# Weight loads in program order, side work fenced behind low halves, and three sets of transposes moved from TensorE to VectorE with a bounce through DRAM

## The chip, the cores and the metric

One core of one Trainium2 chip runs the kernel. The metric is the device time in microseconds (us) of one execution. PE is TensorE (matmuls and transposes by matmul), DVE is VectorE, ACT is ScalarE, POOL is GpSimd and SP is SyncE; SP and POOL only issue DMAs in most of this kernel.

## What is computed

One layer of a streaming encoder on 256 frames of width 2048, all in float32, cut here to what matters:

```
h  = rms_norm(x);  p = h @ w_in            # columns: x_m 1024 | out gate 1024 | u 512 | branch gates 4096
xc = silu(conv4(x_m)); q, k = xc per head; v = x_m per head     # 4 heads of 256
hcell = chunkwise mLSTM(q, k, v, gates)    # matrix memory with max stabiliser
y_m = (sigmoid(o_pre) * (norm(hcell) * g + skip * xc)) @ w_up_m
s   = associative scan of 32 groups x 64 complex states of u    # S5
y   = gelu(Re(C s) + D u);  y_s = (y * sigmoid(y @ w_glu + b)) @ w_up_s
x   = x + (sigmoid(g_m) * y_m + sigmoid(g_s) * y_s) @ w_out
h2  = rms_norm(x);  x = x + (silu(h2 @ w_gate) * (h2 @ w_up)) @ w_down
out = rms_norm(x)
```

## The kernel before

The weights come in 432 blocks of 128x1024 float32 (512 KB). Each block B0 to B431 takes the same way: SP loads it into a tile `raw` (`emit_dma`), ACT casts it to float32r as `hi`, DVE subtracts `lo = raw - hi` (`emit_split`), and PE multiplies it in three passes, xh·hi, xh·lo and xl·hi, where xh and xl are the same split of the activations: 12 matmuls of 128x512 for a block (24 of 128x256 for the first chunk and for the q, k, v and glu blocks). There are three raw, three hi and three lo buffers; the split of a block is emitted two blocks ahead of its matmuls, its load five ahead. In the FFN every fourth raw lies in the pool u8 instead, which has ten buffers of its own.

The order of blocks: the input projection's chunk 4 (the S5 input u, B0 to B7), chunks 0 and 1 (x_m), branch gates with v, q and k between (v is B40 and B41, q B50 and B51, k B60 and B61), chunks 2 and 3 (the output gate), the other gates. The glu blocks B107 and B108 stand three blocks before the end of the last gate chunk, whose last three blocks are B109 to B111. B112 to B119 project S5's output up (`ups_mm`), B120 to B135 the mLSTM's (`upm_mm`), B136 to B167 are w_out, and the FFN begins at FFN0 = B168.

Beside this main row two generators carry the branches: `s5_gen` (scan, output matmuls `y_mm`, GELU, glu) and the mLSTM's `ml_gen`. After each block `pump` lets them emit steps worth a budget of DVE time; the numbers that a step yields are its cost on DVE, its cost on PE and how many blocks must pass before the next. At some places a block needs the result and calls `until`, which emits all that is missing at once. The compiler then schedules each engine's instructions by their dependences: the row on an engine need not be the row of emission, and work without an order between may overtake. Once emitted, each engine runs its row strictly in order. `tc.issue_after(x)` lets what is emitted under it stand only behind instruction x on its engine. Before the change, pump used it in one place only, for S5 steps behind the last of the gates' instructions (`state["fence"]`).

S5's last stretch are the "fix products": 32 elementwise DVE instructions of 128x960 on `stm` and `bu`, in four quarters; behind each quarter eight matmuls of `y_mm` (`aux<-bu,s5sp`, two groups), an addition into `s5ud`, and after the second and the fourth quarter GELU. The split of that, `ghl`, is what the glu blocks multiply.

PE also transposes by matmul with the identity: v (16 of 128x128, into `vtok`), and in `ml_gen`'s last part the heads' output `hc` and the output gate `so` (32). For the merged branches and for x1 the kernel transposes otherwise: DVE transposes 32x32 blocks (`blocks_T`), and POOL's queue writes the tile to DRAM and reads it back in four pieces that put the blocks in place (`groups_dma`, the bounce).

Of the kernel before, what the change touches and what calls it, by code (L numbers as in the profile page):

```python
# [13 lines left out]
AF = mybir.ActivationFunctionType  # L14
# [3 lines left out]
P = 128  # L18
# [22 lines left out]
NTAIL = 5  # L41
# [6 lines left out]
def block_kernel(ctx: ExitStack, tc: tile.TileContext, d, out):  # L48
    nc = tc.nc
# [35 lines left out]
    def aux():  # L85
        return pp.tile([P, 512], F32, tag="aux", name=nm("aux"), bufs=4)
# [6 lines left out]
    def TT(o, a, b, op):  # L93
        return V.tensor_tensor(o, a, b, op=op)  # L94
# [7 lines left out]
    def f(ap):  # L102
        return ap.bitcast(F32)
# [27 lines left out]
                blocks.append((d[name][n, kp], fn_maker, (n, kp)))  # L131

    raws, splits = {}, {}
    wdma = [None]

    def emit_dma(i):
        if i < len(blocks):
            if i == 3:
                raw = u32([P, 1024], name="raw")
            elif FFN0 + 4 <= i < len(blocks) - NTAIL - 4 and i % 4 == 3:  # L140
                raw = u8([P, 1024], name="raw")
            else:
                raw = wp.tile([P, 1024], F32, tag="raw", name=nm("raw"), bufs=NRAW)
            wdma[0] = nc.sync.dma_start(raw, blocks[i][0]).ins
            raws[i] = raw

    def emit_split(i):
        if i < len(blocks):
            raw = raws.pop(i)
            if i >= len(blocks) - NTAIL:  # L150
                hl = u8([P, 2, 1024], F32R, name="hl")
                hi, lo = hl[:, 0], hl[:, 1]
            else:
                hi = wp.tile([P, 1024], F32R, tag="hi", name=nm("hi"), bufs=NHI)
                lo = wp.tile([P, 1024], F32R, tag="lo", name=nm("lo"), bufs=NHI)
            A.copy(hi, raw)  # L156
            TT(lo, raw, f(hi), SUB)
            splits[i] = (hi, lo)

    def o2_block(acc, lhs, kts, hi, lo, first, last):  # L160
# [47 lines left out]
    def pump(i, budget, share, pe=PEB):  # L208
        debt[0] += budget + side_pe[0]
        side_pe[0] = 0.0  # L210
        debt[2] += pe
        while debt[0] > 0 and debt[2] > 0:
            live = [g for g in gens if not g.done and g.ok <= i]
            if not live:
                break
            if len(live) == 2 and debt[1] > 0:
                live.reverse()
            c = None
            for g in live:
                if g is gens[0] and "fence" in state:  # L220
                    with tc.issue_after(state["fence"]):
                        c = g.step()
                else:
                    c = g.step()
                if c:
                    break
                g.ok = i + 1
            if not c:
                break
            dv, p, lat = (tuple(c) + (0, 0))[:3] if isinstance(c, tuple) else (c, 0.0, 0)  # L230
            g.ok = i + lat
            debt[0] -= dv
            debt[2] -= p
            side_pe[0] += p
            debt[1] += dv * (1 - share) if g is gens[0] else -dv * share
        debt[0] = min(debt[0], 0.0)
        debt[2] = min(debt[2], 0.0)
        debt[1] = max(-3.0, min(3.0, debt[1]))
# [39 lines left out]
    def groups_dma(dt_, st_):  # L278
        w = st_.shape[2]
        bounce = dp_.tile([P, 4, w], F32, tag=f"d{w}", name=nm("bounce"))  # L280
        nc.gpsimd.dma_start(bounce, st_)  # L281
        for j in range(4):
            nc.gpsimd.dma_start(  # L283
                dt_[32 * j : 32 * j + 32], bounce.rearrange("(i r) j x -> r i j x", i=4)[:, :, j]
            )


    s5 = {}
# [240 lines left out]
    def ml_gen():  # L529
# [38 lines left out]
        vk = u16([P, 2, 2048], name="vk")  # L568
        ml["vk"] = vk
        vtok = vk[:, 0].rearrange("p (a b) -> p a b", a=2)  # L570
        for st in range(2):
            for e4 in range(2):
                ps_ = aux()
                for e in range(4):
                    PE.transpose(ps_[:, e * 128 : e * 128 + 128], vT[:, e4 * 4 + e, st * 128 : st * 128 + 128], ident)
                A.copy(vtok[:, st, e4 * 512 : e4 * 512 + 512], ps_)
                yield 0.05, 0.45, e4
        gt = cp.tile([P, 2, 8], F32, name="gt")


# [5 lines left out]

        def gate_part(i, src, base):
            gs = m2([P, 256])
            nc.gpsimd.memset(gs, 0.0)
            ps_ = aux()  # L590
            for c in range(8):
                r = 32 * (c % 4)
                mm(ps_[r : r + 8, 0:256], wif[:, i * 8 + c, :], src[:, c, :], c < 4, c >= 4)
            for r in range(0, 128, 32):
                A.copy(gs[r : r + 8, :], ps_[r : r + 8, 0:256])
            yield 0.05, 1.2, 1
            pg = aux()
            for tt in range(2):
                mm(pg[:, tt * 8 : tt * 8 + 8], gs[:, tt * 128 : tt * 128 + 128], sel, True, True)
            TT(gt, pg[:, 0:16].rearrange("p (a b) -> p a b", a=2), base, ADD)  # L600
            yield 0.2, 0.4

        yield from gate_part(2, vT, pvs("bif").unsqueeze(1).broadcast_to([P, 2, 8]))
        del vT
        yield 0.2
        xch = u8([P, 8, 256], F32R, name="xch")
        xcl = u8([P, 8, 256], F32R, name="xcl")
# [14 lines left out]
        qT = ml["q"]  # L622
        yield from gate_part(0, qT, gt)
        yield 0.2
        while "k" not in state:
            yield 0
        yield 0.01, 0, 1
# [18 lines left out]
            STT(rc, rc, c, w2, ADD, MUL)  # L646
        STT(rc, rc, 1.0, w, ADD, MUL)
        TS(v3(lf), fg, 0.0, None, MIN)
        state["fence"] = STT(lf, rc, -2.0, lf, MUL, ADD).ins
        yield 2.6  # L650
        state["gates"] = 1
        mneg = cp.tile([P, 4, 2], F32, name="mneg")
# [5 lines left out]
        for hp in range(2):  # L658
# [79 lines left out]
            yield 0.01, 0.65, 1  # L738
            for pT, h in zip(pTs, hh2):
                nps = aux()  # L740
                vs = lambda st: vtok[:, st, h * 256 : h * 256 + 256]
                mm(nps[:, 0:256], pT[:, 0], vs(0), True, True)
                mm(nps[:, 256:512], pT[:, 1], vs(0), True, False)
                mm(nps[:, 256:512], pT[:, 2], vs(1), False, True)
                for tt in range(2):
                    o = hc[:, 2 * h : 2 * h + 2, tt, :]
                    nv = nps[:, tt * 256 : tt * 256 + 256].rearrange("p (a b) -> p a b", a=2)
                    A.activation(o, nv, AF.Copy, scale=dinv[:, h, tt : tt + 1])
                    jk = m2([P, 2, 128])
                    A.activation(jk, o, AF.Square, accum_out=ssh[:, h, tt : tt + 1])  # L750
                yield 0.01, 1.3, 0
# [5 lines left out]
        for h in range(4):  # L757
            for tt in range(2):
                o = hc[:, 2 * h : 2 * h + 2, tt, :]
                A.activation(o, o, AF.Copy, scale=rsh[:, h, tt : tt + 1])  # L760
        yield 0.6, 0, 3
        while "win" not in state:
            yield 0
        so = ml["so"]
        oh = u8([P, 8, 256], F32R, name="oh")
        ol = u8([P, 8, 256], F32R, name="ol")
        for c2 in range(4):
            hps, sps = aux(), aux()
            for src, ps_ in ((hc, hps), (so, sps)):
                for cc in range(2):  # L770
                    for tt in range(2):
                        ct = 2 * c2 + cc
                        c = (cc * 2 + tt) * 128
                        PE.transpose(ps_[:, c : c + 128], src[:, ct, tt, :], ident)  # L774
            t = m2()
            for cc in range(2):
                ct = 2 * c2 + cc
                ts_ = t[:, cc * 256 : cc * 256 + 256]
                A.activation(ts_, xcT[:, ct, :], AF.Copy, scale=pvs("skip", ct))
                STT(ts_, hps[:, cc * 256 : cc * 256 + 256], pvs("mh", ct), ts_, MUL, ADD)  # L780
            TT(t, t, sps, MUL)
            v2 = lambda a: a[:, 2 * c2 : 2 * c2 + 2, :].rearrange("p a b -> p (a b)")
            A.copy(v2(oh), t)
            TT(v2(ol), t, f(v2(oh)), SUB)
            yield 2.1, 0.9, 1
        ml["out"] = (oh, ol)
        state["out"] = 1
        yield 0.1
# [11 lines left out]
    def win_evac(n, acc):  # L800
# [17 lines left out]
                state["xm"] = 1  # L818
        elif n < 4:
            if n == 2:  # L820
                ml["so"] = u8([P, 8, 2, 128], name="so")
            for tt in range(2):
                A.activation(
                    ml["so"][:, 4 * (n - 2) : 4 * (n - 2) + 4, tt, :],
                    acc[tt].rearrange("p (a b) -> p a b", a=4),
                    AF.Sigmoid,
                    scale=r1[:, tt : tt + 1],
                )
            if n == 3:
                state["so"] = 1  # L830
        else:
            c = n - 5
            key, cc = ("gm", c) if c < 4 else ("gs", c - 4)
            if c == 0:
                mlg.until("heads")
            if cc == 0:
                cur[key] = u16([P, 2, 2048], name=key)
            bg = cur["bg"]
            for tt in range(2):
                o = gate_ap(key, tt, cc)  # L840
                STT(o, acc[tt], r1[:, tt : tt + 1], bg, MUL, ADD)
                A.activation(o, o, AF.Sigmoid)
# [518 lines left out]
```

## Time and profile before

| | |
|---|---|
| median of 3 runs | 1253.72 us (1252.34 to 1253.78) |
| the profiled execution's own time | 1254.09 us |
| its span | 1252.2 us |
| granted TensorE clock, mean | 0.997 of full |
| PE busy | 1231.2 us (98%), 5738 matmuls |
| DVE busy | 804.8 us (64%) |
| ACT busy | 604.5 us (48%) |
| POOL busy | 106.7 us (9%) |
| DMA moved | 258.19 MB, 206 GB/s mean |

The span runs from the first to the last instruction in the trace; the execution's own time lies some 2 us above it. Matmuls are pipelined: one of 128x512 lasts 390 ns in the trace, while the next starts long before its end, so a pace is read from the chain of work, which merges a run of matmuls into a start, a length and a count, and not from single durations. DVE's instructions overlap by about a tenth of a microsecond too. Idle time on an engine counts only where PE waits for it.

### The profile page before, as it was taken

The page shows a single profiled execution, that of the slowest core. Times are in us where ns is not written, and L with a number is a line of the kernel's source. Part 1 is how long each engine was busy: PE and PEld are TensorE (multiplying, and loading weights), DVE is VectorE, ACT ScalarE, POOL GpSimd, SP SyncE. Part 2 cuts the span into 40 slices and gives each one's busy share as a digit, 9 for nine tenths or more (in the row PEclk, how much of TensorE's full clock was granted, in tenths as well). Part 3 has the DMA queues.
Part 4 walks back from the last instruction along what each step waited for, and adds up shares of the span by engine and source line. Part 5 has one row for each costly group of instructions (what it writes and reads, how often), then busy time and mean ns, then how long its engine had stood idle before and what let it go on. Part 6 is the DMA issues. An engine that isn't in the chain of part 4 may idle for free.

```text
span 1252.2 us, 15688 instructions
## 1 busy us (share of the span) xinstructions
PE 1231.2 (98%) x5738; PEld 1015.3 (81%) x5738; DVE 804.8 (64%) x1162; ACT 604.5 (48%) x752; POOL 106.7 (9%) x199
## 2 busy tenths in 40 slices
PE   7999999999999999989999999999999999999997
PEld 7877888887788888878888888888888888888885
DVE  8779945899877857646555555655555554554544
ACT  7574554546754445545344444444444443443433
POOL 0000000000000513201101101110111010000000
PEclk9999999999999999999999999999999999999999
DMA  7645655544565888877767766655765686666453
GB/s 264 208 134 185 193 179 190 169 152 150 180 192 179 274 272 280 281 258 224 218 205 227 221 216 210 195 192 197 242 227 183 220 286 193 204 194 201 149 162 141
DMA packets 75597, 258.19 MB, mean 206 GB/s; under 512 B 10496, under 2 KB 11264, under 8 KB 75520
## 3 DMA queue, kind: packets, MB, share of 16 engines
q1 hardware_dynamic: 67616, 237.25, 59.0%
q0 software_dynamic: 7904, 19.94, 4.9%
q8 instruction: 45, 0.74, 0.2%
q14 instruction: 32, 0.26, 0.1%
HBM read 245.09 MB, written 12.06 MB: 205 GB/s over the span
## 4 chain that ended last, share of the span: by engine, by line
PE 90%; DVE 4%; DMA 3%; issue 1%; ACT 1%; POOL 0%; ACTq 0%; SPq 0%; DVEq 0%
PE acc L100 85%; PE aux L100 4%; DVE lo L94 2%; DMA raw<-in_w_out_dram 1%; DMA raw<-in_w_ffn_gate_dram 1%; DVE xcT L97 1%; ACT hi L156 1%; DVE stm L94 1%; DVE bu L94 0%; DMA m<-bounce 0%; DMA raw<-in_w_in_dram 0%; POOL m L283 0%; PE aux L774 0%; DVE xcT L94 0%; DVE x L94 0%
## 5 line engine op out<-in xcount | busy, mean ns | idle before, releaser
L94 DVE TENSOR_TENSOR lo<-raw,hi 128x1024 fp32r<-128x1024 f32 x427 | 521.8, 1223 | 395.8 <-ACT hi L156 395.1
L156 ACT CAST hi<-raw 128x1024 fp32r<-128x1024 f32 x427 | 449.7, 1054 | 571.9 <-PE acc L100 494.1
L100 PE MATMUL acc<-lo,h2h 128*128 128x512 f32 x704 | 274.5, 390 | 0.5 <-DVE lo L94 0.5
L100 PE MATMUL acc<-hi,h2l 128*128 128x512 f32 x704 | 274.5, 390 | 0.0
L100 PE MATMUL acc<-hi,h2h 128*128 128x512 f32 x704 | 246.3, 390 | 2.6 <-ACT hi L156 2.6
L100 PE MATMUL acc<-hi,aT 128*128 128x512 f32 x664 | 204.6, 389 | 0.0
L100 PEld LDWEIGHTS acc<-hi,h2h 128*128 128x128 f32 x704 | 132.6, 188 | 30.5 <-ACT hi L156 3.1
L100 PEld LDWEIGHTS acc<-lo,h2h 128*128 128x128 f32 x704 | 132.4, 188 | 28.6 <-DVE lo L94 1.0
L100 PE MATMUL acc<-lo,hTh 128*128 128x512 f32 x384 | 153.6, 400 | 1.3 <-DVE lo L94 1.2
L100 PEld LDWEIGHTS acc<-hi,h2l 128*128 128x128 f32 x704 | 132.5, 188 | 27.5
L100 PE MATMUL acc<-hi,hTl 128*128 128x512 f32 x384 | 150.5, 392 | 0.0
L100 PEld LDWEIGHTS acc<-hi,aT 128*128 128x128 f32 x664 | 124.6, 188 | 26.0
L100 PE MATMUL acc<-hi,hTh 128*128 128x512 f32 x384 | 139.4, 393 | 0.0
L100 PE MATMUL acc<-lo,aT 128*128 128x512 f32 x332 | 129.1, 389 | 0.0
L100 PEld LDWEIGHTS acc<-lo,hTh 128*128 128x128 f32 x384 | 72.1, 188 | 22.2 <-DVE lo L94 4.0
L100 PEld LDWEIGHTS acc<-hi,hTh 128*128 128x128 f32 x384 | 71.7, 188 | 16.7 <-issue 2.0
L100 PEld LDWEIGHTS acc<-hi,hTl 128*128 128x128 f32 x384 | 72.2, 188 | 14.6 <-issue 0.7
L281 POOL DMA_DIRECT2D bounce<-m x30 | 17.0, 566 | 690.5 <-DVE m L274 688.5
L100 PEld LDWEIGHTS acc<-lo,aT 128*128 128x128 f32 x332 | 62.3, 188 | 12.8
L283 POOL DMA_DIRECT2D m<-bounce x120 | 65.7, 554 | 44.3 <-DMA bounce<-m 27.3
L100 PE MATMUL acc<-lo,mTh 128*128 128x512 f32 x128 | 49.9, 390 | 0.5 <-DVE lo L94 0.5
L100 PE MATMUL acc<-hi,mTl 128*128 128x512 f32 x128 | 49.8, 389 | 0.0
(246 smaller groups left out, 1078.4 us busy)
## 6 DMA issues: line engine op xcount, KB each, us to landing
raw<-in_w_in_dram SPq DMA_DIRECT2D x104, 512.0 KB, 3.5
raw<-in_w_ffn_gate_dram SPq DMA_DIRECT2D x88, 512.0 KB, 4.1
raw<-in_w_ffn_up_dram SPq DMA_DIRECT2D x88, 512.0 KB, 4.4
raw<-in_w_ffn_down_dram SPq DMA_DIRECT2D x88, 512.0 KB, 4.1
raw<-in_w_out_dram SPq DMA_DIRECT2D x32, 512.0 KB, 4.9
raw<-in_w_up_m_dram SPq DMA_DIRECT2D x16, 512.0 KB, 3.6
bounce<-m POOLq DMA_DIRECT2D x30, 256.0 KB, 4.3
m<-bounce POOLq DMA_DIRECT2D x120, 64.0 KB, 4.2
```

What stands on the lines that cost most here:

```text
L94: return V.tensor_tensor(o, a, b, op=op)
L97: return V.scalar_tensor_tensor(out=o, in0=a, scalar=s, in1=b, op0=op0, op1=op1, **kw)
L100: return PE.matmul(o, l, r, start=start, stop=stop, skip_group_check=True)
L156: A.copy(hi, raw)
L281: nc.gpsimd.dma_start(bounce, st_)
L283: nc.gpsimd.dma_start(dt_[32 * j : 32 * j + 32], bounce.rearrange("(i r) j x -> r i j x", i=4)[:, :, j])
```

## The change

1. **Loads.** Every load of a weight block is ordered behind the load of the block before it. Raws in the pool u8 begin at FFN0 + 20 instead of FFN0 + 4.
2. **Side work.** Each step that pump emits stands behind `vlast`, the low half emitted last (that is, of the block two ahead). The single fence at the gates goes. Steps emitted in `until` are not bound.
3. **Transposes.** v, the heads' output and the output gate are transposed as the other tensors are: 4 bounces each (`bounce_T`: one DVE transpose, one write, four reads), 12 in all, instead of 48 matmuls and four ACT copies. The bounce leaves frames in another order, and the matmuls and products that read the tiles take permuted views. v's bounces stand behind q's gate sums, so v's own tile lives until then. The memset of the gate sums moves from POOL to DVE.

```
-    wdma = [None]
+    wdma, vlast = [None], [None]
-            elif FFN0 + 4 <= i < len(blocks) - NTAIL - 4 and i % 4 == 3:
+            elif FFN0 + 20 <= i < len(blocks) - NTAIL - 4 and i % 4 == 3:
-            wdma[0] = nc.sync.dma_start(raw, blocks[i][0]).ins
+            with tc.issue_after(wdma[0]) if wdma[0] else ExitStack():
+                wdma[0] = nc.sync.dma_start(raw, blocks[i][0]).ins
-            TT(lo, raw, f(hi), SUB)
+            vlast[0] = TT(lo, raw, f(hi), SUB).ins
-                if g is gens[0] and "fence" in state:
-                    with tc.issue_after(state["fence"]):
-                        c = g.step()
-                else:
+                with tc.issue_after(vlast[0]):
                     c = g.step()
+    def bounce_T(o, i):
+        st_ = m2([P, 4, 4, 32])
+        V.transpose(st_.rearrange("p j a c -> p a j c"), i.rearrange("p a (j c) -> p a j c", j=4))
+        groups_dma(o.rearrange("p (i x) -> p i x", i=4), st_.rearrange("p j a c -> p j (a c)"))
...
-                for e in range(4):
-                    PE.transpose(ps_[:, e * 128 : e * 128 + 128], vT[:, e4 * 4 + e, st * 128 : st * 128 + 128], ident)
-                A.copy(vtok[:, st, e4 * 512 : e4 * 512 + 512], ps_)
...
-            nc.gpsimd.memset(gs, 0.0)
+            V.memset(gs, 0.0)
...
         yield from gate_part(0, qT, gt)
         yield 0.2
+        for st in range(2):
+            for e4 in range(2):
+                bounce_T(vtok[:, st, e4 * 512 : e4 * 512 + 512], vT[:, 4 * e4 : 4 * e4 + 4, st * 128 : st * 128 + 128])
+                yield 0.75
...
-        state["fence"] = STT(lf, rc, -2.0, lf, MUL, ADD).ins
+        STT(lf, rc, -2.0, lf, MUL, ADD)
...
-        yield 0.6, 0, 3
+        yield 0.6, 0, 1
+        hcd = u8([P, 2, 2, 512], name="hcd")
+        for hh in range(2):
+            for tt in range(2):
+                bounce_T(hcd[:, hh, tt], hc[:, 4 * hh : 4 * hh + 4, tt, :])
+                yield 0.75
+        yield 0.01, 0, 3
...
-            hps, sps = aux(), aux()
-            for src, ps_ in ((hc, hps), (so, sps)):
-                for cc in range(2):
-                    for tt in range(2):
-                        PE.transpose(ps_[:, c : c + 128], src[:, ct, tt, :], ident)
...
-                STT(ts_, hps[:, cc * 256 : cc * 256 + 256], pvs("mh", ct), ts_, MUL, ADD)
-            TT(t, t, sps, MUL)
+                tv = ts_.rearrange("p (i c) -> p i c", c=32)
+                STT(tv, dv_(hcd, ct), pvs("mh", ct), tv, MUL, ADD)
+                TT(tv, tv, dv_(so, ct), MUL)
...
-                A.activation(
-                    ml["so"][:, 4 * (n - 2) : 4 * (n - 2) + 4, tt, :],
...
+                sg = t2()
+                A.activation(sg, acc[tt], AF.Sigmoid, scale=r1[:, tt : tt + 1])
+                bounce_T(ml["so"][:, n - 2, tt], sg.rearrange("p (a c) -> p a c", a=4))
```

The change moves instructions as well. In these rows a name's number only tells tiles apart, and one number does not mean the same tile before and after.

DVE, at the low half of B109, before the change. `lo_3189`, `lo_3207` and `lo_3232` belong to B107, B108 and B109, `ghl` is the split that glu multiplies:

```order
L94 TENSOR_TENSOR lo_3189<-raw_3116,hi_3188 128x1024
L97 SCALAR_TENSOR_TENSOR t_3263<-t_3263,s5ud 128x512
L94 TENSOR_TENSOR lo_3207<-raw_3136,hi_3206 128x1024
L94 TENSOR_TENSOR ghl_3271<-s5ud,ghl_3271 128x512
L94 TENSOR_TENSOR lo_3232<-raw_3164,hi_3231 128x1024
L94 TENSOR_TENSOR lo_3305<-raw_3186,hi_3304 128x1024
L94 TENSOR_TENSOR s5ud<-s5ud,sgt_3270 128x512
```

DVE at the same low half after the change; it is `lo_3284` now, and the low half of B110 is `lo_3382`:

```order
L94 TENSOR_TENSOR lo_3284<-raw_3213,hi_3283 128x1024
L94 TENSOR_TENSOR bu_668<-bu_668,stm_930 128x64x15 x2
L94 TENSOR_TENSOR stm_930<-s5sp_166 128x960 x2
L94 TENSOR_TENSOR bu_668<-bu_668,stm_930 128x64x15
L97 SCALAR_TENSOR_TENSOR s5ud<-s5ud,pv,aux_3291 128x256
L94 TENSOR_TENSOR lo_3382<-raw_3231,hi_3381 128x1024
L94 TENSOR_TENSOR bu_668<-bu_668,stm_930 128x64x15
L94 TENSOR_TENSOR stm_930<-s5sp_166 128x960
L91 TENSOR_SCALAR t_3305<-t_3305 128x512
L94 TENSOR_TENSOR stm_930<-s5sp_166 128x960
L94 TENSOR_TENSOR bu_668<-bu_668,stm_930 128x64x15
L94 TENSOR_TENSOR t_3305<-t_3305,s5ud 128x512
```

Both halves of `ghl` stood ahead of B109's low half before; now fix products stand behind it (five ahead of B110's low half, six ahead of B111's, five ahead of B112's and two behind that), and `ghl` comes later still.

PE, at the end of B106 before the change. `hi_3166` is B106, `hi_3188` is B107, the first glu block:

```order
L100 MATMUL acc_3123<-hi_3166,hTh_79 128x512
L100 MATMUL acc_3123<-lo_3167,hTh_79 128x512
L100 MATMUL acc_3123<-hi_3166,hTl_81 128x512
L100 MATMUL aux_3276<-ghl_3271,hi_3188 128x256
L100 MATMUL aux_3277<-ghl_3271,hi_3188 128x256
L100 MATMUL aux_3276<-ghl_3271,hi_3188 128x256
```

PE after the change, further on, at the end of B111 (`hi_3415`); B107 is `hi_3233` now:

```order
L100 MATMUL acc_3178<-hi_3415,hTh_79 128x512
L100 MATMUL acc_3178<-lo_3416,hTh_79 128x512
L100 MATMUL acc_3178<-hi_3415,hTl_81 128x512
L100 MATMUL aux_3330<-bu_668,s5sp_166 32x256 x4
L100 MATMUL aux_3353<-ghl_3348,hi_3233 128x256 x2
L100 MATMUL aux_3353<-ghl_3348,lo_3234 128x256
```

B107 has moved from behind B106 to behind B111 and the fifth of six groups of `y_mm` that now stand between B106 and B108; B108 follows the sixth.

SP, at the entry to the FFN before the change. `raw_4726` is the block whose matmuls come next behind those of `raw_4702`; the five between lie in the pool u8:

```order
L144 DMA raw_4684<-in_w_ffn_gate_dram 128x1024
L144 DMA raw_4702<-in_w_ffn_gate_dram 128x1024
L144 DMA raw_4788<-in_w_ffn_up_dram 128x1024
L144 DMA raw_4868<-in_w_ffn_up_dram 128x1024
L144 DMA raw_4942<-in_w_ffn_up_dram 128x1024
L144 DMA raw_5022<-in_w_ffn_gate_dram 128x1024
L144 DMA raw_5117<-in_w_ffn_gate_dram 128x1024
L144 DMA raw_4726<-in_w_ffn_gate_dram 128x1024
```

SP at the same place after the change:

```order
L145 DMA raw_4725<-in_w_ffn_gate_dram 128x1024
L145 DMA raw_4743<-in_w_ffn_gate_dram 128x1024
L145 DMA raw_4767<-in_w_ffn_gate_dram 128x1024
L145 DMA raw_4799<-in_w_ffn_up_dram 128x1024
L145 DMA raw_4829<-in_w_ffn_up_dram 128x1024
```

The loads now stand in the order in which their blocks are used.

## Rows read from the trace of the kernel before

**Rows 1.** The page, busy time by engine: us, share of the span, instructions.

```profile
PE 1231.2 (98%) x5738; PEld 1015.3 (81%) x5738; DVE 804.8 (64%) x1162; ACT 604.5 (48%) x752; POOL 106.7 (9%) x199
```

**Rows 2.** PE's waits: who waited for whom, us in total, times, longest.

```profile
PE acc L100 <- ACT hi L156: 9.7, 2, 7.1
PE acc L100 <- DVE lo L94: 2.3, 3, 1.2
```

**Rows 3.** The chain that ended last: start us, us, what, count.

```profile
313.62 0.57 PE aux L100 x8
...
349.80 5.27 PE aux L100 x44
...
370.27 0.87 PE aux L774 x8
...
524.04 10.86 DMA raw<-in_w_ffn_gate_dram
...
537.36 705.97 PE acc L100 x3106
```

**Rows 4.** Windows of 50 us: length, busy us by engine, PEclk, DMA share, GB/s.

```profile
250.00:300.00 50.00, 50.00 (x244) 41.51 (x243) 49.16 (x129) 24.59 (x41) 0.00 (x0) 1.00 0.50 156
300.00:350.00 50.00, 50.00 (x259) 37.82 (x257) 44.65 (x54) 37.39 (x61) 0.00 (x0) 1.00 0.53 171
```

**Rows 5.** Timeline, DVE and PE: start us, us, operation, count [idle before it <-releaser].

```profile
97.59 1.23 DVE L94 TENSOR_TENSOR xml<-xmT,xmh 128x1024 fp32r<-128x1024 f32 x1
...
100.02 0.50 PE L100 MATMUL acc<-lo,hTh 128*128 128x512 f32 x1 [1.23 <-DVE lo L94]
...
536.10 0.73 PE L100 MATMUL acc<-hi,h2h 128*128 128x512 f32 x2 [2.63 <-ACT hi L156]
537.36 0.50 PE L100 MATMUL acc<-lo,h2h 128*128 128x512 f32 x1 [0.52 <-DVE lo L94]
```

**Rows 6.** Windows of 5 us behind the entry to the FFN.

```profile
535.00:540.00 5.00, 3.38 (x10) 2.43 (x11) 2.59 (x3) 3.04 (x3) 0.00 (x0) 0.82 1.03 293
540.00:545.00 5.00, 5.00 (x20) 4.00 (x19) 3.59 (x6) 3.36 (x6) 0.00 (x0) 0.84 0.83 268
```

**Rows 7.** Groups of DVE instructions by form: count | busy us, mean ns | idle before.

```profile
L94 DVE TENSOR_TENSOR bu<-bu,stm 128x960 f32<-128x960 f32 x16 | 18.4, 1152 | 0.0
L94 DVE TENSOR_TENSOR stm<-s5sp 128x960 f32<-128x960 f32 x16 | 18.4, 1153 | 0.0
```

**Rows 8.** Timeline of DVE, two fix products in a row.

```profile
289.16 1.15 DVE L94 TENSOR_TENSOR bu<-bu,stm 128x960 f32<-128x960 f32 x1
290.23 1.15 DVE L94 TENSOR_TENSOR stm<-s5sp 128x960 f32<-128x960 f32 x1
```

**Rows 9.** Timeline from the last `y_mm` addition to B112.

```profile
338.61 0.47 DVE L97 SCALAR_TENSOR_TENSOR s5ud<-s5ud,pv,aux 128x256 f32<-128x256 f32 x1
...
348.42 0.62 ACT L508 CAST ghl<-s5ud 128x512 fp32r<-128x512 f32 x1
...
348.84 0.64 PE L100 MATMUL aux<-ghl,hi 128*128 128x256 f32 x4
...
349.08 0.69 DVE L94 TENSOR_TENSOR ghl<-s5ud,ghl 128x512 fp32r<-128x512 f32 x1 [0.45 <-ACT ghl L508]
...
354.39 0.84 ACT L929 ACTIVATE sgt<-aux,pv 128x256 f32<-128x256 f32 x2 [1.23 <-PE aux L100]
...
363.74 0.62 PE L100 MATMUL acc<-hi,ghl 128*128 128x512 f32 x2
```

**Rows 10.** Timeline: copies of the gate sums, and two block transposes.

```profile
178.43 1.49 ACT L595 COPY m<-aux 8x256 f32<-8x256 f32 x4
...
402.40 1.30 DVE L274 STREAM_TRANSPOSE m<-gm 128x512 f32<-128x512 f32 x2
```

**Rows 11.** DMA issues of the bounces: count, KB each, median us to landing.

```profile
bounce<-m POOLq DMA_DIRECT2D x30, 256.0 KB, 4.3
m<-bounce POOLq DMA_DIRECT2D x120, 64.0 KB, 4.2
```

More of the change, by code (lines that the diff above doesn't have):

```diff
@@ L570, in ml_gen @@
         vtok = vk[:, 0].rearrange("p (a b) -> p a b", a=2)
-        for st in range(2):
-            for e4 in range(2):
-                ps_ = aux()
-                for e in range(4):
-                    PE.transpose(ps_[:, e * 128 : e * 128 + 128], vT[:, e4 * 4 + e, st * 128 : st * 128 + 128], ident)
-                A.copy(vtok[:, st, e4 * 512 : e4 * 512 + 512], ps_)
-                yield 0.05, 0.45, e4
         gt = cp.tile([P, 2, 8], F32, name="gt")
@@ L603, in ml_gen @@
         yield from gate_part(2, vT, pvs("bif").unsqueeze(1).broadcast_to([P, 2, 8]))
-        del vT
         yield 0.2
@@ L624, in ml_gen @@
         yield 0.2
+        for st in range(2):
+            for e4 in range(2):
+                bounce_T(vtok[:, st, e4 * 512 : e4 * 512 + 512], vT[:, 4 * e4 : 4 * e4 + 4, st * 128 : st * 128 + 128])
+                yield 0.75
+        del vT
         while "k" not in state:
@@ L740, in ml_gen @@
                 nps = aux()
[L741 to L744, printed above, removed]
+                vs = lambda st: vtok[:, st, (h // 2) * 512 : (h // 2) * 512 + 512].rearrange(
+                    "p (i a c) -> p a i c", i=4, a=4
+                )[:, 2 * (h % 2) : 2 * (h % 2) + 2]
+                no = lambda t: nps[:, t * 256 : t * 256 + 256].rearrange("p (a i c) -> p a i c", a=2, i=4)
+                mm(no(0), pT[:, 0], vs(0), True, True)
+                mm(no(1), pT[:, 1], vs(0), True, False)
+                mm(no(1), pT[:, 2], vs(1), False, True)
                 for tt in range(2):
@@ L766, in ml_gen @@
         ol = u8([P, 8, 256], F32R, name="ol")
+        dv_ = lambda d_, ct: d_[:, ct // 4].rearrange("p t (i a c) -> p a (t i) c", i=4, a=4)[:, ct % 4]
         for c2 in range(4):
-            hps, sps = aux(), aux()
-            for src, ps_ in ((hc, hps), (so, sps)):
-                for cc in range(2):
-                    for tt in range(2):
-                        ct = 2 * c2 + cc
-                        c = (cc * 2 + tt) * 128
-                        PE.transpose(ps_[:, c : c + 128], src[:, ct, tt, :], ident)
             t = m2()
@@ L784, in ml_gen @@
             TT(v2(ol), t, f(v2(oh)), SUB)
-            yield 2.1, 0.9, 1
+            yield 2.4, 0, 0
         ml["out"] = (oh, ol)
@@ L820, in win_evac @@
             if n == 2:
-                ml["so"] = u8([P, 8, 2, 128], name="so")
+                ml["so"] = u8([P, 2, 2, 512], name="so")
             for tt in range(2):
-                A.activation(
-                    ml["so"][:, 4 * (n - 2) : 4 * (n - 2) + 4, tt, :],
[L825 to L828, printed above, removed]
+                sg = t2()
+                A.activation(sg, acc[tt], AF.Sigmoid, scale=r1[:, tt : tt + 1])
+                bounce_T(ml["so"][:, n - 2, tt], sg.rearrange("p (a c) -> p a c", a=4))
             if n == 3:
```

## The prediction

> **What bounds the kernel now.** I read the page's busy table first: the matmul engine, PE, is busy 1231.2 us of a span of 1252.2 [rows 1], so a change pays only by taking work off PE or by ending one of its waits, and it costs where it makes PE wait. The waits say where those are: 9.7 us in two waits for the high half (ACT's cast), 7.1 of them at the start, and 2.3 us in three for the low half (VectorE's, DVE's, subtraction) [rows 2]. The chain of waits gives PE's pace: 3106 matmuls in 705.97 us, 227 ns each, so a block of 12 takes 2.73 us; eight transposes 0.87 us, 109 ns each; a group of S5 output matmuls 0.57; 44 glu matmuls of 256 columns 5.27, 120 ns each [rows 3]. DVE by windows shows what could come late: 49.16 us busy of 50 from 250 to 300, 44.65 in the next 50 [rows 4]. In that stretch DVE has no idle time to catch up in.
>
> **Part 1: weights loaded in order.** At the entry to the FFN the next weight block took 10.86 us to land [rows 3]. In the queue before, five far-ahead raws stand in front of it; in the queue after, none. PE waited 2.63 and then 0.52 us there [rows 5], and its granted clock then fell between its levels of 2.4 and 1.2 GHz: 0.82 and 0.84 of full in two windows of 5 us, a loss of 0.9 + 0.8 = 1.7 [rows 6]. If the block lands with its neighbours, all goes: **-4.85 us**. Between 0 (the traffic was the cause, not the order) and -4.85 I take the latter, since the block overtaken is the one that PE waited for.
>
> **Part 2: side work behind its block's low half.** Side work of DVE that the pump emits now stands behind the low half two blocks ahead. One wait is of just this kind: a split of 128x1024 at 97.59 ran ahead of a low half, and PE waited 1.23 us [rows 5]. It goes: **-1.23**. The third, the 0.5 that is left of the 2.3, lies in the output projection, where no pump work is left, and stays.
>
> The other side of this part is the largest term. Before, the S5 branch's work could move ahead into DVE's gaps; now each piece stays behind a low half. The last 32 big pieces, products of 128x960, take 1.15 us each, and one starts 1.07 after the other [rows 7, 8]. Before, all 32 stand ahead of the low half of B109; after, 18 stand behind it, and the S5 matmul groups go with them: PE's row is B106, B109, B110, B111, and only then B107 and B108, the glu blocks, which need the finished S5 output. B107 and B108 meanwhile hold two of three hi/lo buffers, so B109 to B112 pass one buffer in turn: a low half starts only after the block before it is done, and side work stands between. Let T be PE's end of B106. The walk:
> - B109: cast 1.05, low half, matmuls: done at T + 5.2.
> - Behind its low half 5 products and a small step (5.8 us; the small steps last 0.47 to 0.69 [rows 9], each started a tenth before the last ends), then B110's low half; B110 done at T + 12.2.
> - 6 products and 1.0 of others, the low half: B111 done at T + 20.8. 5 products and 1.7 of others, the low half of B112, 2 products, the last group of S5 matmuls: T + 29.4. As a check: 18 x 1.07 = 19.3, others 3.0, three low halves 3.5, from T + 2.4, and 0.57: T + 28.8.
> - Then a chain with no PE work to cover it: GELU and its split. Before, it ran from 338.61 to 349.77, 11.2 us, with four low halves (1.22 each) between its steps [rows 7, 9]; without these 6.3. Two gate evacuations stand in it now: I take 6.9, T + 36.3.
> - What is left of B108 (24 matmuls at 120 ns, nearly all) 2.8; sigmoids 2 x 0.84, a product 0.69, a cast 0.62 [rows 9]: B112 starts at about T + 42.3.
>
> Before, the same way, from the first glu matmul at 348.84 to B112's first at 363.74, took 14.9 [rows 9]. The difference is 27.4. Six groups of S5 matmuls, 3.4 us, were done ahead of T before and lie in these 42.3 now, so T itself comes 3.4 earlier: net **+24.0**. What hid the chain before was that DVE had done S5 by then; with that cover gone nothing else is at hand, since B112 itself needs the result. Bounds: 11.2 for the chain as it ran gives +28; if the scheduler's row lets DVE run ahead in PE's waits as far as buffers allow, and two thirds of the stall remain, +16.
>
> PE's waits in this stretch are longer than the one at the FFN, so the clock should fall there as well: 1.7 lost per place [rows 6], in one to four places, partly under DVE's work: **+3**, between 0 and 7.
>
> **Part 3: transposes off PE.** 48 transposes leave PE: 16 of v, 32 of the heads' output and gate. At 109 ns [rows 3] this is 5.2 us: 1.74 at v; 0.9 lies inside the 14.9 above and is counted there; 24 x 0.109 = 2.6 behind it. **-1.74 and -2.6**, less what the bounces cost. The Trainium skill ("TensorE: Matmul & The Clock Gate", Part 4: PE-mode transpose) gives some 275 ns for one in a kernel's context, by which 48 would be 13.2 us and the sum 8 lower; the trace has that as one transpose's duration, but they overlap, and the measured spacing decides. The same notes ("VectorE: DVE Perf Modes", The three transpose paths) say that VectorE transposes only within 32x32 blocks; here that is the 12 added transposes, each with a write and four reads through HBM.
>
> The 12 DVE transposes take 0.65 each (two in 1.30 [rows 10]), 7.8 us. Eight fall where DVE has gaps; the heads' four come before B109's stretch and push S5 back further, which the row already contains. Bounces: 4.3 us to land for a write, 4.2 for a read [rows 11], with blocks of 2.73 between issue and use: hidden, as the existing 30 are. Their issue is POOL's, an otherwise idle queue. Bound: one late bounce would cost up to 8.5. The v bounces hold v's tile longer, and q's gate sum moves later, with its four ACT copies (1.49 us [rows 10]) under 4 matmuls (0.91): **+0.8** with the write's lag, between 0 and 3.
>
> **The sum**, on the profiled execution's own 1254.09 (0.4 above the median 1253.72): -4.85 - 1.23 + 24.0 + 3 - 1.74 - 2.6 + 0.8 = +17.4: 1271.5. I say **1271**.
>
> **Rivals.**
> - *No stall at glu* (faster). The mechanism is the same place: DVE catches up before B106 ends, because S5 pieces that need nothing from PE run in DVE's waits for casts. For it: DVE is busy only 44.65 of 50 from 300 to 350, 5.3 us of gaps [rows 4]. Against it: an engine runs its row in order, and the 18 products stand behind B109's low half, which needs B106's buffer. It decides at the point where the last S5 group ends by T + 3 or so. Then: 1254.09 - 4.85 - 1.23 - 1.74 - 0.9 - 2.6 + 0.8 = 1243.6. Chance 0.12.
> - *A smaller stall.* Half of the walk's, 12 us and no clock loss: B109 to B111 cover more of DVE's work than I count. 1243.6 + 12 = 1255.6, in bounds 1250 to 1262. Chance 0.17.
> - *The entry to the FFN doesn't mend*: the 10.86 us were traffic, since the bounces of the normalised input run there too. The forecast plus 4.85: 1276. Within the forecast's range; chance 0.2 of it.
> - *Another wait that I don't see*, such as a late v or head bounce (8.5), on top of the forecast: 1280 and more. Chance 0.08.
>
> **How the numbers follow.** Forecast, 1262 to 1280: 0.63. 0.2% is 2.5 us, about what a measurement of this kernel can tell from no change. The first rival is faster; of the second about 0.05 lies within 2.5 us of 1253.72 and 0.02 below; all else is slower: faster 0.14, same 0.05, slower 0.81. The range leaves out the first rival and the top: 1252 to 1281.
>
> **What the profile after would show.** PE's waits name low halves around B109 to B112, some 25 us in all, where before there is none; DVE is busy right through 345 to 372; the first matmul on B112 is about 42 us behind B106's end; the granted clock dips there. No wait of 2.6 at the FFN's entry, a landing of some 4 us there. L774 and L575 rows are gone. Wrong would be: PE busy through the glu stretch, or the low half of B109 with idle DVE time behind it; then my walk has charged products that ran earlier.

## The result

The changed kernel takes 1270.56 us in the median of 4 runs (1269.77 to 1272.38), the kernel before 1253.75 beside it: a ratio of 1.0136, with a 95% interval of 1.0122 to 1.015. The forecast was 1271, slower, and lay within 0.5 us. Where the time went is nearly as forecast; what causes it is only half of what the prediction made its cause.

The page of the changed kernel, first the span, then busy time by engine, and in the third line the granted clock in 40 slices of the span:

```profile
span 1268.6 us, 15707 instructions
...
PE 1230.1 (97%) x5690; PEld 1013.2 (80%) x5690; DVE 815.0 (64%) x1181; ACT 602.4 (47%) x748; POOL 138.7 (11%) x256
...
PEclk9999999999978999999999999999999999999998
```

PE was busy 1231.2 us before [rows 1], so its busy time has hardly changed, although 48 transposes are gone (5690 records against 5738): the matmuls at the lower clock, shown below, fill it up again. The span is 16.4 us longer, and that is idle PE. PE's waits after (us in total, times, longest), against the two lines of [rows 2]:

```profile
PE acc L100 <- ACT hi L157: 8.4, 3, 7.3
PE acc L100 <- DVE lo L94: 7.6, 5, 2.5
PE aux L100 <- ACT ghl L512: 6.6, 1, 6.6
PE aux L100 <- DVE bu L94: 3.5, 3, 1.7
PE acc L100 <- ACT ghl L524: 2.4, 1, 2.4
PE aux L100 <- ACT m L592: 0.5, 1, 0.5
```

The 7.3 is the start. The last line is q's gate sum, which the change moved: 0.5. Two waits for low halves, 1.77 and 0.63, come at 307 and 317, ahead of the stretch that the prediction walks through. All else, 18.7 us, stands between 342 and 387, where there was no wait before.

The timeline of PE (start, length, operation, count, idle before it and what ended it), first the wait at 307, then the stretch with the ends of B106, B110 and B111:

```profile
307.45 0.50 PE L100 MATMUL acc<-lo,hTh 128*128 128x512 f32 x1 [1.77 <-DVE lo L94]
...
342.09 0.39 PE L100 MATMUL acc<-hi,hTl 128*128 128x512 f32 x1
...
352.43 0.50 PE L100 MATMUL acc<-lo,hTh 128*128 128x512 f32 x1 [2.53 <-DVE lo L94]
...
355.48 0.63 PE L100 MATMUL acc<-hi,hTl 128*128 128x512 f32 x1
...
360.92 0.80 PE L100 MATMUL acc<-lo,hTh 128*128 128x512 f32 x1 [1.56 <-DVE lo L94]
...
364.44 0.39 PE L100 MATMUL acc<-hi,hTl 128*128 128x512 f32 x1
...
371.25 0.64 PE L100 MATMUL aux<-bu,s5sp 128*32 128x256 f32 x8 [1.75 <-DVE bu L94]
378.50 1.31 PE L100 MATMUL aux<-ghl,hi 128*128 128x256 f32 x3 [6.61 <-ACT ghl L512]
...
383.88 0.41 PE L100 MATMUL aux<-ghl,lo 128*128 128x256 f32 x1
386.64 0.50 PE L100 MATMUL acc<-hi,ghl 128*128 128x512 f32 x1 [2.35 <-ACT ghl L524]
```

And DVE's: the last of the heads' four transposes ahead of the low half that PE waits for at 307, then the stretch, with hardly a gap between DVE's instructions up to 372:

```profile
304.14 0.72 DVE L288 STREAM_TRANSPOSE m<-hc 128x512 f32<-128x512 f32 x1
...
306.17 1.23 DVE L94 TENSOR_TENSOR lo<-raw,hi 128x1024 fp32r<-128x1024 f32 x1
...
351.16 1.22 DVE L94 TENSOR_TENSOR lo<-raw,hi 128x1024 fp32r<-128x1024 f32 x1
...
368.86 2.34 DVE L94 TENSOR_TENSOR bu<-bu,stm 128x960 f32<-128x960 f32 x2
...
372.25 0.47 DVE L97 SCALAR_TENSOR_TENSOR s5ud<-s5ud,pv,aux 128x256 f32<-128x256 f32 x1
...
376.52 1.41 DVE L97 SCALAR_TENSOR_TENSOR gm<-acc,r,t 128x512 f32<-128x512 f32 x2 [0.56 <-DMA t<-in_bg_dram]
378.48 0.69 DVE L94 TENSOR_TENSOR ghl<-s5ud,ghl 128x512 fp32r<-128x512 f32 x1 [0.55 <-ACT ghl L512]
```

The fix products end at 371.20; in the kernel before the last ended at 332.5. Here an engine off the bound, DVE, holds back the bound one, and its busy share of the whole span (64% before and after) tells nothing of that.

For all kernels the same three points are read from PE's timeline: T, the end of B106 (its last matmul's start, 342.09 in the changed kernel, + 0.23); the first matmul of B112; and the first of the FFN. The spans between them add up to the execution:

| kernel | T | T to B112 | B112 to FFN | FFN to end | span |
|---|---|---|---|---|---|
| before | 348.85 | 14.89 | 155.97 | 732.49 | 1252.2 |
| changed | 342.32 | 44.32 | 154.12 | 727.85 | 1268.6 |
| difference | -6.53 | +29.43 | -1.85 | -4.64 | +16.4 |

### The profile page after: what moved, and what is told of

It is laid out like the page before. It is cut to its first block, busy times and chain, and to the rows that moved or that the text cites. A ratio compares the mean times of both kernels' runs of the same rounds, so it can differ in the third digit from the quotient of the medians.

```text
span 1268.6 us, 15707 instructions
## 1 busy us (share of the span) xinstructions
PE 1230.1 (97%) x5690; PEld 1013.2 (80%) x5690; DVE 815.0 (64%) x1181; ACT 602.4 (47%) x748; POOL 138.7 (11%) x256
## 4 chain that ended last, share of the span: by engine, by line
PE 85%; issue 8%; DVE 3%; DMA 2%; ACT 1%; POOL 1%; SPq 0%; ACTq 0%; POOLq 0%; DVEq 0%
PE acc L100 82%; PE aux L100 2%; DMA bounce<-m 1%; DVE bu L94 1%; DVE lo L94 1%; DVE stm L94 1%; POOL vk L281 0%; ACT hi L157 0%; DMA so<-bounce 0%; DMA raw<-in_w_in_dram 0%; POOL so L281 0%; DMA t<-in_bg_dram 0%; ACT m L783 0%; PE aux L547 0%; ACT L844 0%
## 5 line engine op out<-in xcount | busy, mean ns | idle before, releaser
L279 POOL DMA_DIRECT2D bounce<-m x42 | 23.6, 563 | 765.1 <-DVE m L272 496.1
```

## The experiments

Each time is a median; the kernel before, run beside them, stood at 1253.87, 1254.07 and 1253.85. "Behind" a low half means later in DVE's row.

**Part 1 alone.** The kernel before with the loads of the change.

```
-            elif FFN0 + 4 <= i < len(blocks) - NTAIL - 4 and i % 4 == 3:
+            elif FFN0 + 20 <= i < len(blocks) - NTAIL - 4 and i % 4 == 3:
...
-            wdma[0] = nc.sync.dma_start(raw, blocks[i][0]).ins
+            with tc.issue_after(wdma[0]) if wdma[0] else ExitStack():
+                wdma[0] = nc.sync.dma_start(raw, blocks[i][0]).ins
```

> The kernel before with part 1 alone (loads in program order, u8 raws from FFN0 + 20). Theory, the load that was overtaken: the waits of 2.63 and 0.52 us at the entry to the FFN and the 1.7 us of half clock behind them go, 1253.7 - 4.85 = about 1249; nothing else moves. Rival, the traffic of the entry and not the order was the cause: 1253 to 1254, with a wait of 2 us or more left there.

Measured: 1249.14, ratio 0.9963 (0.995 to 0.9976). Its PE waits:

```profile
PE acc L100 <- ACT hi L157: 7.5, 1, 7.5
PE acc L100 <- DVE lo L94: 1.5, 2, 1.2
```

The high half has only the start's wait left. What stood ahead of the block in the queue was the cause, and the term of 4.85 is right (4.7). The run changes the order and the later start of the u8 raws together, so it does not say which of the two does it. T to B112 is 14.89 here as before.

**Part 2 alone.** The kernel before with pump's steps behind `vlast`.

```
-            TT(lo, raw, f(hi), SUB)
+            vlast[0] = TT(lo, raw, f(hi), SUB).ins
...
-                if g is gens[0] and "fence" in state:
-                    with tc.issue_after(state["fence"]):
-                        c = g.step()
-                else:
+                with tc.issue_after(vlast[0]):
                     c = g.step()
```

> The kernel before with part 2 alone (pump's side work behind the low half of the block two ahead). 5 of the 32 fix products stand behind the low half of B109, against 18 in the changed kernel and none before, and the second half of ghl behind that of B113. Theory, the stall goes by the DVE work that is left behind T (the end of B106): 5 products, an addition, three low halves, 11 us, then the chain of 6.9, what is left of B108 and 3.1 more, less the PE work of B109 to B111 and B107, B108: a stall of 10 to 16 us, less 1.23 for the wait that goes: 1262 to 1268. Rival, the fence alone makes the whole stall of the changed kernel: 1275 to 1279.

Measured: 1265.51, ratio 1.0099 (1.0081 to 1.0117), within the theory's range. T to B112 is 32.29.

**Part 3 alone.** The kernel before with `bounce_T` for v, the heads' output and the gate; pump and loads as before.

> The kernel before with part 3 alone (v, heads' output and gate by DVE and the bounce; pump as before). 1 of the fix products stands behind the low half of B109, but the second half of ghl stands behind that of B113 here too, since 8 more transposes of 0.65 us stand on DVE ahead of it. Theory, the added DVE work too pushes S5 back: 5.2 us of PE's transposes go, but a chain of GELU, glu and ghl with only 22 matmuls beside it costs 6 to 10: 1254 to 1259. Rival, the bounces are hidden and only the fence makes a stall: 1253.7 - 5.2 + 0.5 = 1249.

Measured: 1268.08, ratio 1.0118 (1.0102 to 1.0133). The rival is out, but the theory's own number was too low by 9. T to B112 is 30.03. PE's waits:

```profile
PE acc L100 <- ACT hi L156: 9.5, 3, 6.9
PE acc L100 <- ACT ghl L526: 4.5, 1, 4.5
PE acc L100 <- DVE lo L94: 4.4, 7, 1.2
PE aux L100 <- ACT ghl L514: 3.2, 1, 3.2
```

DVE's timeline behind T (349.0) shows the work that came between:

```profile
348.95 1.67 DVE L97 SCALAR_TENSOR_TENSOR m<-hcd,pv,m 128x256 f32<-128x256 f32 x4
...
358.02 1.15 DVE L94 TENSOR_TENSOR bu<-bu,stm 128x960 f32<-128x960 f32 x1
...
362.31 0.48 DVE L97 SCALAR_TENSOR_TENSOR s5ud<-s5ud,pv,aux 128x256 f32<-128x256 f32 x1
...
369.61 0.68 DVE L94 TENSOR_TENSOR ghl<-s5ud,ghl 128x512 fp32r<-128x512 f32 x1
```

I had counted fix products only. The heads' products with `so` and `hcd` and three low halves stand between the last products too, so these end at 359.2, T + 10, and GELU's chain then lasts from 362.31 to 370.3, 8 us, followed by glu's at the lower clock.

**The changed kernel with slack 0.** One number: pump hands out 0.3 us more of side work per block.

```
-SLACK = 0.3
+SLACK = 0.0
```

> The changed kernel with one number changed: the slack that pump leaves on DVE in every block is 0 instead of 0.3 us, so that S5's and the mLSTM's steps are emitted earlier, by 0.3 us of work for each of some 86 blocks, 26 us in all. No fix product stands behind the low half of B109 then, and B107 comes right behind B106. Theory, the stall is only late S5 work: it goes, and the three gains are left, 1253.7 - 4.85 - 1.23 - 5.2 + 0.5 = 1243, perhaps 1 to 3 more for tighter blocks ahead. Rival, DVE is full in B60 to B106 and the work taken earlier only makes PE wait there: 1255 to 1268.

Measured: 1238.92, ratio to the kernel before 0.988 (0.9863 to 0.9896). It beats both kernels, and the theory's number by 4. Its only PE waits in the whole span:

```profile
PE acc L100 <- ACT hi L157: 7.5, 1, 7.5
PE acc L100 <- DVE lo L94: 0.6, 1, 0.6
```

T is 344.06, T to B112 13.94, 0.95 under the kernel before: the eight transposes that lay there. With the side work handed out earlier no stall is left, so the stall was its lateness on DVE.

**The changed kernel without part 2.** Pump as before.

> The changed kernel without part 2: pump as before, with loads in order and the bounces. 1 fix product stands behind the low half of B109, the second half of ghl behind that of B113. Theory, the lateness of S5 is a sum over DVE and the parts are independent but for it: as part 3 alone (1268.1), less the 4.7 that the loads gave alone: 1262 to 1265, with the stretch from B106's end to B112 at 30 us as there. Rival, the fence is what makes the changed kernel slow: without it only gains are left, 1245 to 1250.

Measured: 1263.16, ratio 1.0081 (1.0061 to 1.0101); T to B112 29.89. As part 3 alone less the loads' 4.7 (1263.4). Taking the fence out gives back 7 of the 17 us.

**The glu blocks at the end of the gate chunk.**

```
-GLU = 3
+GLU = 0
```

> The changed kernel with the glu blocks at the end of the last gate chunk (they become B110 and B111) and not three blocks ahead of it, so that they hold no hi/lo buffers while gate blocks wait. The 18 fix products still stand behind the low half of B109. Theory, the sum of DVE's late work sets B112, not the buffers: the last S5 matmuls still end some 29 us behind B106, then 6.9, 2.9 and 3.1: stretch 41 to 44, time 1267 to 1272. Rival, the buffers that B107 and B108 hold make the gate blocks slow: stretch 28 to 34, time 1253 to 1260.

Measured: 1272.44, ratio 1.0158 (1.0136 to 1.018); T to B112 46.57. One line of its waits:

```profile
PE aux L100 <- DVE bu L94: 14.7, 3, 5.8
```

That is 0.4 over the theory's range in time and 2.6 in the stretch, and far from the rival. With hi and lo buffers free, the gate blocks hardly wait; PE waits for the fix products instead. The two buffers that B107 and B108 hold, which the walk names, do not set the end; the sum on DVE does.

**Slack 0.15.** Half way.

> The changed kernel with pump's slack at 0.15 us, half way between 0.3 (1270.6) and 0 (1238.9): 13 us more of side work before the glu blocks. 3 fix products stand behind the low half of B109. Theory, the stall goes by the amount of late work: some 13 us of the stall of 29 are left, 1252 to 1259. Rival, it is a step: what is late at all costs the whole chain, 1265 to 1271.

Measured: 1251.11, ratio 0.9976 (0.9964 to 0.9987), a microsecond under the theory's range and far from the rival: T to B112 is 25.82 and the last fix product ends at 349.7, T + 7, where it was T + 29 with slack 0.3. The stall goes with the late work, not in one step.

**The kernel before with slack 0.**

> The kernel before with pump's slack at 0 and nothing else. S5 was not late there: the fix products end at 332, 16 us ahead of B106's end. Theory, slack 0 gains only by undoing lateness: no gain here, 1252 to 1256, and the gain of the changed kernel with slack 0 is then that of its three parts. Rival, slack 0 is a gain of its own, and the parts give less than they seem to: 1243 to 1250.

Measured: 1255.32, ratio 1.0017 (1.0006 to 1.0029). Its fix products end at 291 instead of 333, and T to B112 is 14.81 as before. Slack is no gain in itself.

**Slack 0 without part 2.**

> The changed kernel with slack 0 and without part 2: what the fence is worth where S5 is not late. Glu, B109 to B111 and B112 stand in plain order, no fix product behind the low half of B106. Theory, the fence is worth the waits that it takes away, 1.2 for the split ahead of a low half and one insertion of S5 input matmuls, 1.1: 1240 to 1243 against 1238.9 with it. Rival, the fence gains nothing by itself or costs, since it holds side work back: 1236 to 1239.

Measured: 1246.30, ratio 0.9939 (0.9914 to 0.9963): the fence is worth 7.4 us where S5 is not late, three times what I expected, and the time is 3.3 over the theory's range. Waits explain 1.9 of it (low halves 2.5 us in four waits, against 0.6). Some of the rest is side matmuls. Without the fence:

```profile
L100 PE MATMUL aux<-s5ud,s5bT 32*128 32x256 f32 x64 | 6.8, 400 | 0.0
L100 PE MATMUL aux<-bu,s5sp 128*32 128x256 f32 x64 | 5.7, 386 | 0.0
```

With it (slack 0, the fastest kernel); count | busy us, mean ns | idle before:

```profile
L100 PE MATMUL aux<-s5ud,s5bT 32*128 32x256 f32 x64 | 5.7, 400 | 0.0
L100 PE MATMUL aux<-bu,s5sp 128*32 128x256 f32 x64 | 4.7, 388 | 0.0
```

The same 64 matmuls of each kind take 1.1 and 1.0 us less, since they stand in fewer, longer runs in PE's row (five against six of the first kind). The other 3 or so are not traced to rows.

**Slack 0 without part 3.**

> The changed kernel with slack 0 and without part 3: the transposes stay on PE. Theory, where S5 is not late a transpose is worth its 109 ns on PE: 1238.9 + 5.2 = 1243 to 1246. Rival, a transpose costs PE some 275 ns, its duration: 1238.9 + 13 = 1250 to 1253.

Measured: 1246.17, ratio 0.9939 (0.9919 to 0.9959), 0.2 over the theory's range: the bounces are worth 7.3 us where S5 is not late, of which 48 x 109 ns make 5.2. The rival, 275 ns each, is out. The stages bear the price out, since PE waits in neither kernel there: the 8 transposes between T and B112 make 0.87 (14.81 against 13.94), 109 ns each, the 24 from B112 to the FFN 2.8 (155.14 against 152.32), 118 each. Without the fence the bounces are worth less, by an estimate: the kernel before with slack 0 (1255.32), less the loads' 4.7, less 1246.30 leaves 4.3.

**Slack -0.15.**

> The changed kernel with slack -0.15 us, 13 us more of side work ahead than with 0: is there more to get by earlier S5 work? With slack 0, PE waits 0.6 us in all behind the first block. Theory, nothing is late any more, and fuller blocks make low halves late: 1239 to 1244. Rival, still earlier is still better: 1236 to 1238.

Measured: 1248.97, ratio 0.9961 (0.9946 to 0.9977): 10 us over slack 0, 5 over the range. Side work handed out early has another limit: PE waits again at the mLSTM's heads, which the pump serves from the same budget (PE, then ACT):

```profile
298.04 0.46 PE L100 MATMUL aux<-m,cst 128*128 128x130 f32 x2 [1.65 <-DVE m L97]
...
321.62 1.06 PE L100 MATMUL acc<-hi,hTh 128*128 128x512 f32 x2 [3.53 <-ACT hi L157]
...
317.33 3.30 ACT L764 ACTIVATE hc<-hc,rsh 128x256 f32<-128x256 f32 x8 [0.64 <-DVE rsh L97]
```

## Why the prediction was right, and where it wasn't

**The loads** (-4.85): -4.64 from the FFN to the end, -4.7 alone. PE runs through the entry at full clock (1.00 in the windows from 535 to 550), so the 1.7 of [rows 6] is gone with the two waits.

**The work ahead of T.** Forecast: -1.23, -1.74, +0.8 and 3.4 moved behind T, -5.6 in all. Measured -6.53. The wait of the split is gone, q's gate sum waits 0.5, and six groups of S5 matmuls moved behind T (3.7). Against the forecast stand the two waits at 307 and 317, 2.4 us: the low half of 306.17 came behind the heads' four transposes, which the prediction had charged to S5 alone, and two gate products; the other came behind two fix products. A run of S5 input matmuls less, 1.1, which I had not looked for, and some 2 us that are not traced to rows make up for them. That this stage is off by 1 us only is luck.

**The walk through the stretch** (42.3, and +3 for the clock) held at its main points, while the steps between were up to 1.6 late: B110 ended at T + 13.6 for 12.2, B111 at T + 22.4 for 20.8. The last S5 matmuls were forecast to end at T + 29.4 and end at 371.9, T + 29.6; the second half of `ghl` lets PE go on at 378.50, T + 36.2, forecast 36.3. The clock's share was the right guess. Windows of 5 us (length, PE busy, ..., PEclk before the last two columns):

```profile
370.00:375.00 5.00, 0.64 (x8) 0.16 (x8) 3.81 (x6) 1.49 (x3) 0.00 (x0) 0.91 0.60 195
375.00:380.00 5.00, 1.50 (x5) 1.28 (x6) 2.80 (x4) 2.97 (x5) 0.00 (x0) 0.50 0.17 64
380.00:385.00 5.00, 4.29 (x21) 4.00 (x19) 0.69 (x1) 1.95 (x4) 0.00 (x0) 0.57 0.00 2
385.00:390.00 5.00, 3.36 (x10) 2.70 (x11) 3.12 (x4) 2.22 (x5) 0.00 (x0) 0.77 0.32 108
390.00:395.00 5.00, 5.00 (x21) 4.03 (x21) 1.71 (x3) 1.05 (x1) 0.00 (x0) 0.89 0.00 0
```

After 6.6 us of waiting, B108 ran near 1.2 GHz (0.50 and 0.57): from 378.50 to 384.1, 5.6 us instead of the 2.8 in the walk. B112 and what follows lost 5 x 0.23 + 5 x 0.11 = 1.7 at most. Together 4.5; the walk had 0.7 us too much in its last steps (3.2 from B108's end to B112, where 2.5 passed), and its 3 came out near the total. Of PE's waits the prediction expected some 25 us, named for low halves; they are 18.7, and 5.2 of these are for low halves of B109 to B111. The others are for the fix products and `ghl`, and matmuls at the lower clock fill part of the time that the walk left empty.

**The transposes behind B112** (-2.6): the stage is 1.85 shorter, where -2.6 and a wait of 0.53 that is gone as well are set against the clock's 1.3 to 1.7 at its head; the prediction had let that wait stand. The price of 109 ns held (109 and 118 in the stages at slack 0). The duration of one, in the kernel before (count | busy us, mean ns | idle before), is another number:

```profile
L774 PE MATMUL aux<-cst,hc 128*128 128x128 f32 x16 | 2.6, 272 | 0.0
```

The Trainium skill ("TensorE: Matmul & The Clock Gate", Part 4) has some 275 ns, for bf16, and the 272 of this trace, for float32, is near it. It is not what a transpose costs PE: the kernel without part 3 is 7.3 us slower at slack 0, not 13.

**The total** is nearer than its parts. By stage the measured span is off the forecast by -1.0 ahead of T, +2.0 from T to B112, +0.8 and +0.2 behind it, and the 3 for the clock, summed apart, lie inside these: -1.0 in all.

**What failed is the cause.** The prediction charged the stall to part 2 and booked part 3 as a gain of 4.3 with hidden bounces, mentioning only in passing that the added DVE work pushes S5 back. Part 3 alone costs 14.2 us, more than part 2 alone with 11.6; without part 2 the kernel is still 9 slower than before. The sum was right because it was walked along DVE's row of the changed kernel, in which both causes stand already. Both make S5 late, and that lateness is shown to be the cause: with slack 0 it goes, and the stall with it. Either alone leaves only 8 (part 2) or 3 (part 3) of the 32 products to end behind T (both together 20), but what comes late then stands in a chain that nothing covers.

Why each makes S5 late is less sure. Pump hands out side work by a budget that leaves DVE 0.3 us per block. That the compiler could move S5 work ahead into it before the change, and that the fence forbids this, is argued and not shown by a run of its own. Part 3's share can be read from DVE's row, and the 7.8 us of its 12 transposes are the smaller part of it. In the kernel before and in part 3 alone S5 stands still on DVE from some 150 us until the last of the gates' instructions, behind which it goes on at 226.4 and 229.4. Before, 13 of its 15 pairs of scan products (`stm<-bu,s5sm`) were done ahead of that; in part 3 alone v's transposes lie there, one with a wait for an earlier bounce, and 11 were. So two groups of them, 5.0 us, come behind the gates. The steps of the mLSTM's second pair of heads, 5.0 us, now stand ahead of the first fix product too. With two transposes (1.2), four more low halves (4.6) and the start 3.0 later, this product comes at 284.8 instead of 265.8, 19.0 us later. The kernel before, then part 3 alone:

```profile
152.88 1.29 DVE L94 TENSOR_TENSOR stm<-bu,s5sm 128x512 f32<-128x512 f32 x2
...
265.79 2.22 DVE L94 TENSOR_TENSOR stm<-s5sp 128x960 f32<-128x960 f32 x2
```

```profile
155.21 0.71 DVE L290 STREAM_TRANSPOSE m<-vT 128x512 f32<-128x512 f32 x1 [2.42 <-DMA bounce<-m]
...
284.83 1.15 DVE L94 TENSOR_TENSOR stm<-s5sp 128x960 f32<-128x960 f32 x1
```

The bounces were thus not hidden from DVE, as the prediction had them, though none of PE's waits names one.

**The rivals.** "No stall" was priced at 1243.6; with the stall's cause taken away the kernel takes 1238.9, so the gains that the change has in itself are larger than I counted by some 5 us (the side effects of the fence and the bounces above).

## What to carry to other kernels

Where a change moves side work, count what stands on the helper's row between the last instruction that the main row waits for and the block that needs the result, in the changed order: that sum and the serial chain behind it gave the end of the last S5 matmuls and of `ghl` within 0.2 us here, while shares of busy time told nothing. A change that orders work more strictly or adds to a helper engine needs the pacing set anew with it: here one constant turned +17 us into -15, and a little more of the same lost 10 again. And the price of a part is its price in company: the same fence costs 11.6 us alone, 7.4 with the bounces at the old pace, and gains 7.4 at the new one.

## What the runs showed of the hardware

- A short run of these small side matmuls has a fixed price on PE: 4 or 16 of `aux<-s5ud,s5bT` take about 1.07 us alike, so that fewer runs are cheaper with the same matmuls (six runs 6.8 us busy, five 5.7). From the chain of the kernel before (start, us, what, count):

```profile
52.90 1.08 PE aux L100 x16
...
61.86 1.06 PE aux L100 x4
```

- The clock had fallen already early in the stretch. Behind waits of 0.57, 1.09 and 0.57 us, from 343 to 349, the granted clock was still full; PE then waited 2.53 and ran a few matmuls, and it fell. Two windows of 5 us of the changed kernel:

```profile
345.00:350.00 5.00, 3.89 (x20) 2.25 (x20) 4.97 (x6) 1.05 (x1) 0.00 (x0) 1.00 0.47 142
350.00:355.00 5.00, 2.57 (x8) 2.05 (x9) 5.00 (x7) 0.63 (x1) 0.00 (x0) 0.86 0.28 89
```

  And from 390 to 395, with PE busy all the time, it was still 0.89. Here the stall cost more than its waits.
